# Layer 2 of a hybrid encoder: the i and z projections written as seven products of half-size quarters, with weight sums added by DMA, and the heads in groups of eight

## The chip, the core and the metric

One core of a Trainium2 chip runs the whole program. The metric is the time of one execution in microseconds (us) on the device. The engines are TensorE (PE; its weight loads are listed as PEld), VectorE (DVE), ScalarE (ACT), GpSimd (POOL) and the queue engine SyncE (SP); each works through its own instructions in a fixed order, and semaphores join them.

## What is computed

Two layers on 512 tokens of width 1024, in float32. The change lies in the second one:

```python
def odd_layer(x, norm_g, w_in, gamma_f, gamma_b, head_norm_g, w_out, layer):
    h = rms_norm(x, norm_g)                                   # 512 x 1024
    proj = h @ w_in                                           # 1024 x 10240
    q, f_f, f_b, i, z = split_cols(proj, [2048] * 5)          # 16 heads of 128 columns each
    q = jax.nn.silu(q)
    o = hgrn2(q, f_f, i, forwards) + hgrn2(q, f_b, i, backwards)
    o = o * lax.rsqrt(jnp.mean(o * o, axis=-1, keepdims=True) + EPS) * head_norm_g
    return (o * jax.nn.silu(z)) @ w_out                       # added to x, then a last rms_norm
```

## The kernel before

**Three products for one.** Every float32 operand of a main product is split into two float32r parts, hi + lo, and a product of two tiles of 128 is three matmuls, hi·hi, hi·lo and lo·hi, of 128 x 512 each. `mm3` issues them into one PSUM bank; its matmuls are the line L207 of the profile. After every eighth matmul `mm3` calls `tick()`, which lets up to three side jobs (attention, gate, recurrence of a head) each come one stage further, so that small matmuls stand between the main ones.

**Weights.** A piece is 512 KB. The class `Weights` holds the list of pieces in the order of use: `_dma` loads one on SP's queue (L49) into one of 4 buffers `wraw`, up to 7 pieces ahead of use; `_split` copies it to `whi` on ACT (L58) and subtracts to `wlo` on DVE (L59), up to 3 pieces ahead of use, 4 buffers each. A buffer `wraw` is free again when DVE has read it.

**Layer 2.** While the last products of layer 1 end tile by tile (four tiles t of 128 tokens), `norm_to_hT` squares each tile on ACT, scales it (one power on POOL, L142; two DVE products, L161), transposes it on PE (L167) and splits it into `hhi`, `hlo` (L170, L171). Then four rounds J follow. Each round has two calls of `nat_blocks`, for i and for z of four heads (512 columns): four pieces are taken, and each tile t gets 8 x 3 = 24 matmuls with all 1024 rows, so a round has 192 for i and z. `evac_i` copies the bank to `iv` on ACT (L718); `evac_z` takes a sigmoid on ACT (L721) and a product on DVE (L722). Then an output product of finished heads, and for each head three `t_block`s (q and two gates, 24 matmuls each) and the side job `hgrn`, of about 16 stages' worth of ticks. In `hgrn` POOL multiplies q (L630, L632) before the scores on PE (L642), and at the end o by z (L701).

What sets the order: the calls below are run once to build the program, a scheduler then fixes the order of each engine, and a queue never passes an instruction that waits.

## Time and profile before

| | us |
|---|---|
| median of 3 timed runs (lowest, highest) | 1036.41 (1036.37, 1037.04) |
| the profiled execution, first to last instruction | 1035.3 |
| PE busy / DVE busy / ACT busy / POOL busy | 1012.9 / 597.7 / 517.1 / 147.4 |
| main matmuls (L207), mean start to start 0.227 | 3792 |

The span leaves out 1.1 us of the timed execution. PE is the engine to watch: it is busy in 98% of the span, and its busy time is that of pipelined rows, so one matmul's listed 0.39 us is not its price; the distance from one start to the next is.

### The profile page before, as it was taken

The page shows a single profiled execution, that of the slowest core. Times are in us where ns is not written, and L with a number is a line of the kernel's source. Part 1 is how long each engine was busy: PE and PEld are TensorE (multiplying, and loading weights), DVE is VectorE, ACT ScalarE, POOL GpSimd, SP SyncE. Part 2 cuts the span into 40 slices and gives each one's busy share as a digit, 9 for nine tenths or more (in the row PEclk, how much of TensorE's full clock was granted, in tenths as well). Part 3 has the DMA queues.
Part 4 walks back from the last instruction along what each step waited for, and adds up shares of the span by engine and source line. Part 5 has one row for each costly group of instructions (what it writes and reads, how often), then busy time and mean ns, then how long its engine had stood idle before and what let it go on. Part 6 is the DMA issues. An engine that isn't in the chain of part 4 may idle for free.

```text
span 1035.3 us, 13564 instructions
## 1 busy us (share of the span) xinstructions
PE 1012.9 (98%) x5381; PEld 851.9 (82%) x5381; DVE 597.7 (58%) x946; ACT 517.1 (50%) x705; POOL 147.4 (14%) x155
## 2 busy tenths in 40 slices
PE   6999999999999999999999999999999999999996
PEld 5888888888888887888888888888888888878884
DVE  6574677566434464446754546754436764547685
ACT  5333666354222144458743258753257753377742
POOL 1140000000000200004231003322002322012101
PEclk9999999999999999999999999999999999999998
DMA  9243222222233222341212432212432223422102
GB/s 322 85 120 85 81 62 62 82 82 82 82 85 99 85 81 82 100 131 54 85 39 82 122 102 62 63 61 82 122 102 61 62 62 102 122 82 77 47 1 81
DMA packets 109343, 90.05 MB, mean 87 GB/s; under 512 B 2992, under 2 KB 88544, under 8 KB 109280
## 3 DMA queue, kind: packets, MB, share of 16 engines
q1 hardware_dynamic: 109184, 89.14, 28.3%
q8 instruction: 42, 0.69, 0.3%
q14 instruction: 21, 0.17, 0.1%
q0 software_dynamic: 96, 0.04, 0.0%
HBM read 87.08 MB, written 2.10 MB: 86 GB/s over the span
## 4 chain that ended last, share of the span: by engine, by line
PE 89%; ACT 3%; DVE 3%; issue 2%; POOL 1%; DMA 1%; SPq 0%; POOLq 0%; DVEq 0%; ACTq 0%
PE mm L207 74%; PE sm L670 2%; PE sm L642 2%; PE sm L448 1%; PE sm L685 1%; PE sm L487 1%; PE sm L691 1%; PE sm L689 1%; DVE c L614 1%; PE sm L476 1%; PE sm L658 1%; PE sm L705 1%; PE sm L512 1%; PE sm L644 1%; ACT whi L58 1%
## 5 line engine op out<-in xcount | busy, mean ns | idle before, releaser
L59 DVE TENSOR_TENSOR wlo<-wraw,whi 128x1024 fp32r<-128x1024 f32 x156 | 196.9, 1268 | 143.9 <-ACT whi L58 141.5
L58 ACT CAST whi<-wraw 128x1024 fp32r<-128x1024 f32 x156 | 163.1, 1051 | 231.2 <-PE mm L207 215.0
L207 PE MATMUL mm<-hlo,whi 128*128 128x512 f32 x656 | 258.2, 394 | 0.0
L207 PE MATMUL mm<-hhi,wlo 128*128 128x512 f32 x656 | 257.8, 393 | 0.0
L207 PE MATMUL mm<-hhi,whi 128*128 128x512 f32 x656 | 256.5, 391 | 0.0
L207 PEld LDWEIGHTS mm<-hhi,whi 128*128 128x128 f32 x656 | 123.3, 188 | 24.6
L207 PEld LDWEIGHTS mm<-hlo,whi 128*128 128x128 f32 x656 | 123.3, 188 | 24.1
L207 PEld LDWEIGHTS mm<-hhi,wlo 128*128 128x128 f32 x656 | 123.3, 188 | 23.9
L207 PE MATMUL mm<-whi,hhi 128*128 128x512 f32 (+1 forms) x352 | 135.9, 386 | 0.1
L207 PE MATMUL mm<-whi,hlo 128*128 128x512 f32 (+1 forms) x352 | 135.5, 385 | 0.0
L207 PE MATMUL mm<-wlo,hhi 128*128 128x512 f32 (+1 forms) x352 | 135.3, 385 | 0.0
L207 PE MATMUL mm<-whi,ahi 128*128 128x512 f32 x256 | 100.4, 392 | 0.1
L207 PE MATMUL mm<-wlo,ahi 128*128 128x512 f32 x256 | 100.3, 392 | 0.0
L207 PE MATMUL mm<-whi,alo 128*128 128x512 f32 x256 | 100.1, 392 | 0.0
L207 PEld LDWEIGHTS mm<-wlo,hhi 128*128 128x128 f32 x352 | 66.6, 189 | 13.1 <-DVE wlo L59 1.1
L207 PEld LDWEIGHTS mm<-whi,hhi 128*128 128x128 f32 x352 | 66.8, 190 | 12.6 <-ACT hhi L170 0.7
L207 PEld LDWEIGHTS mm<-whi,hlo 128*128 128x128 f32 x352 | 66.5, 189 | 12.0 <-DVE hlo L171 0.3
L254 DVE TENSOR_TENSOR x<-mm,x 128x512 f32<-128x512 f32 x72 | 49.0, 688 | 43.5 <-PE mm L207 43.4
L630 POOL TENSOR_TENSOR sq<-sq,en 128x512 f32<-128x512 f32 x14 | 23.8, 1700 | 266.4 <-ACT en L622 266.4
L207 PEld LDWEIGHTS mm<-whi,ahi 128*128 128x128 f32 x256 | 48.1, 188 | 10.2 <-ACT ahi L707 0.5
L207 PEld LDWEIGHTS mm<-whi,alo 128*128 128x128 f32 x256 | 48.1, 188 | 9.6
L207 PEld LDWEIGHTS mm<-wlo,ahi 128*128 128x128 f32 x256 | 48.1, 188 | 9.5
(176 smaller groups left out, 1377.2 us busy)
## 6 DMA issues: line engine op xcount, KB each, us to landing
wraw<-in_w_in_odd_dram SPq DMA_DIRECT2D x80, 512.0 KB, 3.9
wraw<-in_w_in_even_dram SPq DMA_DIRECT2D x44, 512.0 KB, 4.0
wraw<-in_w_out_even_dram SPq DMA_DIRECT2D x16, 512.0 KB, 3.5
wraw<-in_w_out_odd_dram SPq DMA_DIRECT2D x16, 512.0 KB, 3.5
x<-in_x_dram SPq DMA_DIRECT2D x4, 512.0 KB, 8.3
out_dram<-x SPq DMA_DIRECT2D x8, 256.0 KB, 2.1
pThi<-in_norm_g_even_dram SPq DMA_DIRECT2D x1, 512.0 KB, 5.4
lngb<-in_gmlp_ln_g_dram SPq DMA_DIRECT2D x1, 512.0 KB, 6.1
```

Source lines behind the costliest of these rows:

```text
L58: self.nc.scalar.copy(hi, raw)
L59: self.nc.vector.tensor_tensor(out=lo, in0=raw, in1=hi.bitcast(F32), op=ALU.subtract)
L207: nc.tensor.matmul(ps, lhsT=l, rhs=r, start=(i == 0), stop=(i == n - 1))
L254: nc.vector.tensor_tensor(out=xv, in0=ps, in1=xv, op=ALU.add)
L448: nc.tensor.matmul(pv, lhsT=a[:, ql], rhs=b[:, kv, kr], start=(i == 0), stop=(i == 2))
L476: nc.tensor.transpose(ps[:, ts(n - n0, P)], pr[:, n, ts(j - KEYS[n][0], P)], ident)
L487: nc.tensor.matmul(po[:, n0 * P:n1 * P], lhsT=a[:, j, ts(kv, P)], rhs=b[:, j, :w], start=(j == 0 and i == 0), stop=(j == NT - 1 and i == 2 ...
L512: nc.tensor.matmul(ps[:, ts(n, P)], lhsT=va[n][:, ts(c, P)], rhs=wsT[:, g], start=True, stop=True)
L614: nc.vector.tensor_tensor_scan(out=cf, data0=reset.rearrange("p n t -> p (n t)"), data1=cf, initial=0.0, op0=ALU.mult, op1=ALU.add)
L630: eng.tensor_tensor(out=v8(qb), in0=v8(qf), in1=en[:, 1, :, 0:64], op=ALU.mult)
L642: nc.tensor.matmul(ps[:H, o:o + P], lhsT=kf[:, lo_:mid], rhs=qf[:, lo_:hi_], start=True, stop=True)
L670: nc.tensor.matmul(ps[:, ts(2 * j + d, P)], lhsT=kn[:, jj, d], rhs=iv[:, n, hs], start=True, stop=True)
```

## The change

**The products.** A unit j is what a round J had: i and z of four heads, 1024 columns. Tokens, the 1024 rows and the two column halves (i, z) are each cut in two, and seven products of quarters replace eight. A product has 24 matmuls (p = 0, 1, two tiles of tokens, 12 each) and takes two new pieces; a unit has 7 x 24 = 168 instead of 192. A PSUM bank is handed on: product 1 adds onto the bank that product 0 left and that ACT or DVE has read in between (X: products 1, 2; Z: products 3, 4; Y: products 5 to 7). `unit_first` is products 1 and 2, which need only the first two tokens' tiles; `unit_rest` is 3 to 7.

**Sums of activations.** Four sums or differences of the quarters of the normed input ("forms") are made in `norm1`, which replaces `norm_to_hT` there: per p, two DVE differences from PSUM, two more in SBUF, four casts on ACT and four lo parts on DVE, plus copies on ACT. They lie in the buffers `sq`, `sg`, `c`, which the heads need; so eight DMAs of 512 KB write them to DRAM in `units(0)` and eight read them back in `units(2)`.

**Sums of weights.** Of the ten pieces of `unit_rest`, two are plain (b22), two are b12 loaded on SP with b22 added, two are b11 with b12 added ("base" of a chain, buffer `wch`), two are the same buffer with b22 added after its first split, two with b21 added after its second. Each addition is a DMA with accumulation, 512 KB, issued from POOL: 8 a unit, 32 in all. Three buffers `wch` serve eight chains.

**Order.** Two units together, then eight heads: `plan1`. The sigmoid of z now goes to a buffer `sig` and POOL multiplies. The three small loads of `rows` go from POOL's queue to SP's.

```diff
     def add(self, ap):
-        self.src.append(ap)
+        self.src.append((ap, None, None, None))
+    def add_sum(self, ap, plus, chain=None):
+        self.src.append((ap, plus, chain, False))
+    def add_grown(self, plus, chain):
+        self.src.append((None, plus, chain, True))
+    def _plus(self, t, ap):
+        self.nc.gpsimd.dma_start(out=t, in_=ap, accum_op=ALU.add)
     def _dma(self):
-        ap = self.src[self.n_dma]
-        t = self.pool.tile(list(ap.shape), F32, tag="wraw", name="wraw", bufs=self.raw_bufs)
-        self.nc.sync.dma_start(out=t, in_=ap)
-        self.raw[self.n_dma] = t
+        ap, plus, chain, grown = self.src[self.n_dma]
+        if not grown:
+            tag, bufs = ("wch", self.chain_bufs) if chain is not None else ("wraw", self.raw_bufs)
+            t = self.pool.tile(list(ap.shape), F32, tag=tag, name=tag, bufs=bufs)
+            self.nc.sync.dma_start(out=t, in_=ap)
+            if plus is not None:
+                self._plus(t, plus)
+            self.raw[self.n_dma] = t
         self.n_dma += 1
     def _split(self):
         i = self.n_split
-        raw = self.raw.pop(i)
+        _, _, chain, grown = self.src[i]
+        raw = self.chains.pop(chain) if grown else self.raw.pop(i)
         hi = self.pool.tile(list(raw.shape), F32R, tag="whi", name="whi", bufs=self.bufs)
         lo = self.pool.tile(list(raw.shape), F32R, tag="wlo", name="wlo", bufs=self.bufs)
         self.nc.scalar.copy(hi, raw)
         self.nc.vector.tensor_tensor(out=lo, in0=raw, in1=hi.bitcast(F32), op=ALU.subtract)
         self.ready[i] = (hi, lo)
         self.n_split += 1
+        if chain is not None:
+            later = next((p for _, p, c, g in self.src[i + 1:] if c == chain and g), None)
+            if later is not None:
+                self._plus(raw, later)
+                self.chains[chain] = raw
...
+    W.chain_bufs = 3
...
-    def mm3(ps, ops):
+    def mm3(ps, ops, first=True):
         n = len(ops)
         for i, (l, r) in enumerate(ops):
-            nc.tensor.matmul(ps, lhsT=l, rhs=r, start=(i == 0), stop=(i == n - 1))
+            nc.tensor.matmul(ps, lhsT=l, rhs=r, start=(first and i == 0), stop=(i == n - 1), skip_group_check=not first)
...
-    for J in range(4):
-        add_nat(wio, OI1 + J * 512)
-        add_nat(wio, OZ1 + J * 512)
-        if J:
-            add_out(woo, 4 * (J - 1), 2 if J == 3 else 4)
-        for h in range(4 * J, 4 * J + 4):
-            add_tcols(wio, OQ1 + h * P)
-            add_tcols(wio, OF1 + h * P)
-            add_tcols(wio, OB1 + h * P)
+    def quarter(j, kh, nh):
+        c0 = (OI1, OZ1)[nh] + j * 512
+        return [cols(wio[(512 * kh + 256 * p):(512 * kh + 256 * p + 256)], c0, 512) for p in range(2)]
+    def add_unit_first(j):
+        for ap in quarter(j, 0, 0) + quarter(j, 1, 0):
+            W.add(ap)
+    def add_unit_rest(j):
+        b11, b12, b21, b22 = quarter(j, 0, 0), quarter(j, 0, 1), quarter(j, 1, 0), quarter(j, 1, 1)
+        for p in range(2):
+            W.add_sum(b11[p], b12[p], (j, p))
+        for p in range(2):
+            W.add(b22[p])
+        for p in range(2):
+            W.add_grown(b22[p], (j, p))
+        for p in range(2):
+            W.add_sum(b12[p], b22[p])
+        for p in range(2):
+            W.add_grown(b21[p], (j, p))
+    plan1 = [("units", 0), ("heads", 0, 6), ("out", 0, 4), ("heads", 6, 8), ("units", 2), ("heads", 8, 10), ("out", 4, 4), ("heads", 10, 14),
+             ("out", 8, 2), ("heads", 14, 16)]
+    for kind, *i in plan1:
+        if kind == "units":
+            add_unit_first(i[0])
+            add_unit_first(i[0] + 1)
+            add_unit_rest(i[0])
+            add_unit_rest(i[0] + 1)
+        elif kind == "heads":
+            for h in range(*i):
+                add_head(h)
+        else:
+            add_out(woo, *i)
...
-        nc.gpsimd.dma_start(out=rows[32 * d:32 * d + 32], in_=gsrc.rearrange("l (h d) -> (l h) d", d=P))
-    nc.gpsimd.dma_start(out=rows[64:80], in_=hng[0].rearrange("(h d) -> h d", d=P))
+        nc.sync.dma_start(out=rows[32 * d:32 * d + 32], in_=gsrc.rearrange("l (h d) -> (l h) d", d=P))
+    nc.sync.dma_start(out=rows[64:80], in_=hng[0].rearrange("(h d) -> h d", d=P))
...
+    FORM_TAGS = ("sq", "sq", "sq", "sg", "sg", "sg", "c", "c")
+    def form_tiles():
+        f = [l1.tile([P, 4, 256], F32R, tag=g, name="form", bufs=2 if g == "c" else 3) for g in FORM_TAGS]
+        return [(f[2 * i], f[2 * i + 1]) for i in range(4)]
+    forms = form_tiles()
+    r1 = l1.tile([P, 2, 2, 512], F32, tag="zv", name="r1", bufs=2)
+    formed = set()
+    def norm1(t, g, h, ss, wait):
+        p = t % 2
+        r = rstd_halves(ss, "nr")
+        for kq, cs in enumerate(halves):
+            nc.vector.scalar_tensor_tensor(out=h[:, cs], in0=xs[t][:, cs], scalar=r, in1=g[kq], op0=ALU.mult, op1=ALU.mult)
+        yield wait
+        if t >= 2:
+            r22 = l1.tile([P, 512], F32, tag="o2", name="r22", bufs=1)
+            s1 = l1.tile([P, 512], F32, tag="u", name="s1", bufs=1)
+            s3 = l1.tile([P, 512], F32, tag="kn1", name="s3", bufs=1)
+        for kq in (0, 1) if t < 2 else (1, 0):
+            ps = sm_bank()
+            for j in range(4):
+                nc.tensor.transpose(ps[:, ts(j, P)], h[:, ts(4 * kq + j, P)], ident)
+            pv = ps.rearrange("p (j t) -> p j t", j=4)
+            hv = hhi[:, 4 * kq:4 * kq + 4, ts(t, P)]
+            nc.scalar.copy(hv, pv)
+            nc.vector.tensor_tensor(out=hlo[:, 4 * kq:4 * kq + 4, ts(t, P)], in0=pv, in1=hv.bitcast(F32), op=ALU.subtract)
+            if t < 2:
+                nc.scalar.copy(r1[:, p, kq], ps)
+            elif kq == 1:
+                nc.scalar.copy(r22, ps)
+            else:
+                nc.vector.tensor_tensor(out=s1, in0=ps, in1=r22, op=ALU.subtract)
+                nc.vector.tensor_tensor(out=s3, in0=ps, in1=r1[:, p, 0], op=ALU.subtract)
+        normed.add(t)
+        if t < 2:
+            return
+        s2, s4 = r1[:, p, 0], r1[:, p, 1]
+        nc.vector.tensor_tensor(out=s2, in0=s1, in1=s2, op=ALU.subtract)
+        nc.vector.tensor_tensor(out=s4, in0=s4, in1=s2, op=ALU.add)
+        for i, sgn, src in ((0, 1.0, s1), (3, 1.0, s4), (1, 1.0, s2), (2, -1.0, s3)):
+            hi, lo = (f[:, :, ts(p, P)] for f in forms[i])
+            sv = src.rearrange("p (j t) -> p j t", j=4)
+            nc.scalar.activation(hi, sv, AF.Copy, scale=sgn)
+            nc.vector.scalar_tensor_tensor(out=lo, in0=sv, scalar=sgn, in1=hi.bitcast(F32), op0=ALU.mult, op1=ALU.subtract)
+        formed.add(p)
...
-            spawn(norm_to_hT(t, g1, ht[:, t % 2], sst[t], 2))
+            spawn(norm1(t, g1, ht[:, t % 2], sst[t], 2))
...
+    def a_quarter(kh, th):
+        return lambda k, p: [a[:, 4 * kh + k, ts(2 * th + p, P)] for a in (hhi, hlo)]
+    def a_form(i):
+        return lambda k, p: [f[:, k, ts(p, P)] for f in forms[i]]
+    def product(a_of, banks, first, done):
+        pieces = [W.take() for _ in range(2)]
+        for p in range(2):
+            if first:
+                tick_until(lambda: p in normed)
+                banks.append(mm_bank())
+            ops = []
+            for k in range(4):
+                (a, b), (whi, wlo) = a_of(k, p), pieces[k // 2]
+                ops += [(a, whi[:, k % 2]), (a, wlo[:, k % 2]), (b, whi[:, k % 2])]
+            mm3(banks[p], ops, first)
+            done(p, banks[p])
+    def sub(out, a, b):
+        nc.vector.tensor_tensor(out=out, in0=a, in1=b, op=ALU.subtract)
+    def unit_first(iv):
+        X = []
+        product(a_quarter(0, 0), X, True, lambda p, ps: nc.scalar.copy(iv[:, 2 + p], ps))
+        product(a_quarter(1, 0), X, False, lambda p, ps: nc.scalar.copy(iv[:, p], ps))
+    def unit_rest(iv, zv):
+        def silu(t):
+            sig = l1.tile([P, 512], F32, tag="o2", name="sig", bufs=1)
+            nc.scalar.activation(sig, zv[:, t], AF.Sigmoid)
+            nc.gpsimd.tensor_tensor(out=zv[:, t], in0=zv[:, t], in1=sig, op=ALU.mult)
+        def c12(p, ps):
+            sub(zv[:, p], zv[:, p], ps)
+            silu(p)
+        def c22(p, ps):
+            sub(zv[:, 2 + p], zv[:, 2 + p], ps)
+            silu(2 + p)
+        Z, Y = [], []
+        product(a_form(0), Z, True, lambda p, ps: sub(zv[:, 2 + p], ps, iv[:, 2 + p]))
+        product(a_form(3), Z, False, lambda p, ps: sub(zv[:, p], ps, iv[:, 2 + p]))
+        product(a_form(1), Y, True, c12)
+        product(a_form(2), Y, False, c22)
+        product(a_quarter(1, 1), Y, False,
+                lambda p, ps: nc.vector.tensor_tensor(out=iv[:, 2 + p], in0=ps, in1=iv[:, 2 + p], op=ALU.add))
+    ivs, zvs = {}, {}
+    spill = ctx.enter_context(tc.tile_pool(name="spill", bufs=1, space=bass.MemoryType.DRAM))
+    kept = [[spill.tile([P, 4, 256], F32, name=f"form{i}{j}", tag=f"form{i}{j}") for j in range(2)] for i in range(4)]
+    def units(j):
+        nonlocal forms
+        for k in (j, j + 1):
+            ivs[k] = l1.tile([P, NT, 512], F32, tag="iv", name="iv", bufs=2)
+            unit_first(ivs[k])
+        if j:
+            forms = form_tiles()
+            for f, d in zip(forms, kept):
+                for a, b in zip(f, d):
+                    nc.sync.dma_start(out=a.bitcast(F32), in_=b)
+        else:
+            tick_until(lambda: len(formed) == 2)
+            for f, d in zip(forms, kept):
+                for a, b in zip(f, d):
+                    nc.sync.dma_start(out=b, in_=a.bitcast(F32))
+        for k in (j, j + 1):
+            zvs[k] = l1.tile([P, NT, 512], F32, tag="zv", name="zv", bufs=2)
+            unit_rest(ivs[k], zvs[k])
+    def heads(h0, h1):
+        for h in range(h0, h1):
             sq = l1.tile([P, 2, S], F32, tag="sq", name="sq", bufs=3)
             sg = l1.tile([P, 2, S], F32, tag="sg", name="sg", bufs=3)
             ps = t_block()
             for d in range(2):
                 ps = t_block()
                 nc.scalar.activation(sg[:, d], ps, AF.Sigmoid)
-            spawn(hgrn(h, sq, sg, iv, zv))
+            spawn(hgrn(h, sq, sg, ivs[h // 4], zvs[h // 4]))
+    def outs(k0, n):
+        tick_until(lambda: all(k in acat1 for k in range(k0, k0 + n)))
+        out_blocks([acat1[k] for k in range(k0, k0 + n)])
+    for kind, *i in plan1:
+        {"units": units, "heads": heads, "out": outs}[kind](*i)
...
-    nc = _bacc.Bacc("TRN2", target_bir_lowering=False, num_devices=1)
+    nc = _bacc.Bacc("TRN2", target_bir_lowering=False, num_devices=1, dynamic_dma_scratch_size=2048)
```

Three places show how it moves the engines' rows. In the names, `wraw` and `wch` are raw weights, `whi`, `wlo` their parts, `form` a form, `s`, `r` its float32 sources.

DVE where tile 3 (`x_73`) is normed, at the start of layer 2. Before:

```order
L254 TENSOR_TENSOR x_73<-mm,x_73 128x512
L59 TENSOR_TENSOR wlo<-wraw,whi 128x1024
L155 TENSOR_SCALAR nrv<-ss 128x1
L161 SCALAR_TENSOR_TENSOR ht<-x_73,nrr,gain_3031 128x512 x2
L171 TENSOR_TENSOR hlo<-sm,hhi 128x4x128 x2
```

The same engine and place after the change:

```order
L278 TENSOR_TENSOR x_73<-mm,x_73 128x512
L681 TENSOR_TENSOR s_3240<-sm,r_3239 128x512
L682 TENSOR_TENSOR s_3241<-sm,r_3042 128x512
L77 TENSOR_TENSOR wlo<-wraw,whi 128x1024
L687 TENSOR_TENSOR r_3042<-s_3240,r_3042 128x512
L693 SCALAR_TENSOR_TENSOR form<-s_3240,form 128x4x128
L688 TENSOR_TENSOR r_3042<-r_3042 128x512
L693 SCALAR_TENSOR_TENSOR form<-r_3042,form 128x4x128
L77 TENSOR_TENSOR wlo<-wraw,whi 128x1024
L693 SCALAR_TENSOR_TENSOR form<-r_3042,form 128x4x128
L693 SCALAR_TENSOR_TENSOR form<-s_3241,form 128x4x128
L179 TENSOR_SCALAR nrv<-ss 128x1
```

Eight instructions of tile 2's forms and a second weight split now stand between tile 3's last sum and its norm.

POOL from the end of layer 1's norms on. Before:

```order
L142 TENSOR_TENSOR nrr<-nrv,mhalf 128x1 x4
L630 TENSOR_TENSOR sq<-sq,en 128x512
L632 TENSOR_TENSOR sq<-sq,c 128x512
L606 MEMSET c 128x16
L651 TENSOR_TENSOR asum<-asum,ax 64x4x64 x2
```

The same after the change (L57 is the accumulating DMA, L853 the product with the sigmoid):

```order
L166 TENSOR_TENSOR nrr<-nrv,mhalf 128x1 x4
L57 DMA wraw<-in_w_in_odd_dram 128x2x512 x2
L57 DMA wch<-in_w_in_odd_dram 128x2x512 x4
L57 DMA wraw<-in_w_in_odd_dram 128x2x512
L853 TENSOR_TENSOR zv<-zv,sig 128x512
L57 DMA wraw<-in_w_in_odd_dram 128x2x512
L853 TENSOR_TENSOR zv<-zv,sig 128x512 x2
L57 DMA wch<-in_w_in_odd_dram 128x2x512
L853 TENSOR_TENSOR zv<-zv,sig 128x512
L57 DMA wch<-in_w_in_odd_dram 128x2x512 x5
```

Nothing stood on POOL between the norms and the first head's products; now fourteen accumulating DMAs and four products with the sigmoid stand in these rows.

SP's queue at the same place. Before:

```order
L49 DMA wraw<-in_w_out_even_dram 128x2x512 x8
L49 DMA wraw<-in_w_in_odd_dram 128x2x512 x2
L585 DMA gain_3031<-in_norm_g_odd_dram 128x1024
L49 DMA wraw<-in_w_in_odd_dram 128x2x512 x6
L49 DMA wraw<-in_w_in_odd_dram 128x8x128 x12
```

The same after the change:

```order
L64 DMA wraw<-in_w_in_odd_dram 128x2x512 x9
L889 DMA form_3273<-form 128x1024
L889 DMA form_3277<-form 128x1024
L889 DMA form_3274<-form 128x1024
L889 DMA form_3275<-form 128x1024
L889 DMA form_3276<-form 128x1024
L889 DMA form_3278<-form 128x1024
L889 DMA form_3279<-form 128x1024
L889 DMA form_3280<-form 128x1024
L64 DMA wraw<-in_w_in_odd_dram 128x2x512 x4
L64 DMA wch<-in_w_in_odd_dram 128x2x512 x2
```

The eight writes of forms stand before the plain pieces of unit 1 and before the base of the fourth chain, the first of the two `wch` at the end. (The bases of the first three chains are loaded, and summed, far ahead, in layer 1.)

## Rows read from the trace of the kernel before

**Rows 1.** The page: span, and busy time (share of span) and instructions by engine.

```profile
span 1035.3 us, 13564 instructions
...
PE 1012.9 (98%) x5381; PEld 851.9 (82%) x5381; DVE 597.7 (58%) x946; ACT 517.1 (50%) x705; POOL 147.4 (14%) x155
```

**Rows 2.** Waits of PE: waiting line, releaser: us in total, times, longest.

```profile
PE sm L167 <- DVE h L161: 8.2, 3, 7.5
PE sm L642 <- POOL sq L632: 4.1, 4, 1.0
```

**Rows 3.** Timeline of PE in dense main products: start us, us, instruction.

```profile
354.77 0.39 PE L207 MATMUL mm<-whi,alo 128*128 128x512 f32 x1
...
371.77 0.39 PE L207 MATMUL mm<-whi,alo 128*128 128x512 f32 x1
```

**Rows 4.** Windows: length, busy by engine (instructions), granted clock, DMA share, GB/s.

```profile
0.00:25.90 25.90, 17.60 (x73) 13.10 (x74) 16.24 (x25) 14.06 (x27) 3.34 (x12) 1.00 0.90 322
...
393.10:437.60 44.50, 44.24 (x199) 36.02 (x198) 16.10 (x20) 15.94 (x24) 0.55 (x1) 1.00 0.31 94
...
440.00:520.00 80.00, 78.97 (x469) 66.54 (x468) 49.26 (x75) 56.42 (x66) 18.76 (x19) 1.00 0.31 93
```

**Rows 5.** Timeline around tile 3's norm, DVE.

```profile
395.87 0.68 DVE L254 TENSOR_TENSOR x<-mm,x 128x512 f32<-128x512 f32 x1
396.46 1.22 DVE L59 TENSOR_TENSOR wlo<-wraw,whi 128x1024 fp32r<-128x1024 f32 x1
397.60 0.21 DVE L155 TENSOR_SCALAR nrv<-ss 128x1 f32<-128x1 f32 x1
398.46 1.42 DVE L161 SCALAR_TENSOR_TENSOR ht<-x,nrr,gain 128x512 f32<-128x512 f32 x2 [0.66 <-POOL nrr L142]
```

**Rows 6.** Timeline around tile 3's norm, PE.

```profile
392.35 1.03 PE L167 MATMUL sm<-ident,ht 128*128 128x128 f32 x8
393.14 0.48 PE L207 MATMUL mm<-whi,hhi 128*128 128x512 f32 x1
...
399.36 1.29 PE L167 MATMUL sm<-ident,ht 128*128 128x128 f32 x8 [0.21 <-DVE ht L161]
```

**Rows 7.** Groups by line: busy us, mean ns | idle before, releasers.

```profile
L59 DVE TENSOR_TENSOR wlo<-wraw,whi 128x1024 fp32r<-128x1024 f32 x156 | 196.9, 1268 | 143.9 <-ACT whi L58 141.5
L58 ACT CAST whi<-wraw 128x1024 fp32r<-128x1024 f32 x156 | 163.1, 1051 | 231.2 <-PE mm L207 215.0 <-issue 12.6 <-DMA wraw<-in_w_in_even_dram 3.0
...
L722 DVE TENSOR_TENSOR zv<-mm,zv 128x512 f32<-128x512 f32 x16 | 11.0, 690 | 42.4 <-ACT zv L721 42.4
...
L161 DVE SCALAR_TENSOR_TENSOR ht<-x,nrr,gain 128x512 f32<-128x512 f32 x8 | 5.7, 748 | 2.4 <-POOL nrr L142 2.4
...
L542 POOL DMA_DIRECT2D rows<-in_hgrn_gamma_fwd_dram x1 | 0.7, 725 | 0.0
```

**Rows 8.** DMA issues: transfer, queue, count, KB each, median us to landing.

```profile
wraw<-in_w_in_odd_dram SPq DMA_DIRECT2D x80, 512.0 KB, 3.9
...
x<-in_x_dram SPq DMA_DIRECT2D x4, 512.0 KB, 8.3
```

**Rows 9.** The tile zv on POOL: ns min/median/max of one, first and last start.

```profile
L701 POOL TENSOR_TENSOR o<-o,zv x14: 1288/1308/2140, 489.3 to 973.4; 128x512 f32<-128x512 f32 x14
```

More of the change, by code (lines that the diff above doesn't have):

```diff
@@ L40, in __init__ @@
         self.src, self.raw, self.ready = [], {}, {}
+        self.chains = {}
         self.n_dma = self.n_split = self.n_used = 0
     def add(self, ap):
[L44 to L50 removed]
+        self.src.append((ap, None, None, None))
[5 more added lines that the diff above has]
+        self.nc.gpsimd.dma_start(out=t, in_=ap, accum_op=ALU.add)
+    def _dma(self):
+        ap, plus, chain, grown = self.src[self.n_dma]
[6 more added lines that the diff above has]
+            self.raw[self.n_dma] = t
         self.n_dma += 1
@@ L711, in hgrn @@
         yield 1
-    for J in range(4):
-        iv = l1.tile([P, NT, 512], F32, tag="iv", name="iv", bufs=2)
-        zv = l1.tile([P, NT, 512], F32, tag="zv", name="zv", bufs=2)
-        def evac_i(t, ps):
-            nc.scalar.copy(iv[:, t], ps)
-        def evac_z(t, ps):
-            nc.scalar.activation(zv[:, t], ps, AF.Sigmoid)
-            nc.vector.tensor_tensor(out=zv[:, t], in0=ps, in1=zv[:, t], op=ALU.mult)
-        nat_blocks(evac_i)
-        nat_blocks(evac_z)
-        if J:
-            n = 2 if J == 3 else 4
-            tick_until(lambda: 4 * (J - 1) + n - 1 in acat1)
-            out_blocks([acat1[4 * (J - 1) + k] for k in range(n)])
-        for h in range(4 * J, 4 * J + 4):
+    def a_quarter(kh, th):
+        return lambda k, p: [a[:, 4 * kh + k, ts(2 * th + p, P)] for a in (hhi, hlo)]
```

4 lines of the change are left out of this document (added).

## Prediction

> **What bounds the kernel now.** I read the page's first part before anything else: PE is busy in 1012.9 of 1035.3 us and no other engine passes 58% [rows 1]. PE's busy time overlaps itself, so the second view is its waits: apart from 8.2 us at the very start, only 4.1 us in four waits stand against it in the whole span [rows 2]. So nearly every microsecond is a matmul's turn, and a matmul that goes is time that goes. The third view gives its price: between two rows 75 matmuls apart lie 371.77 - 354.77 = 17.00 us, 0.2267 us each [rows 3]. The listed 0.39 us is not the price. The other engines and the DMA engines cost nothing now because they have room: in the i and z block of round J = 0, 44.5 us, DVE works 16.1, ACT 15.9, POOL 0.6, and the DMA engines are 31% busy [rows 4]. That room is what the change spends. The question is whether PE stays fed.
>
> **The change, part by part.**
>
> *Matmuls.* Four units save 24 each: 96 x 0.2267 = **-21.8 us**. No other PE work is added, and the form operands have the tile shapes of the old ones, so I keep the price.
>
> *Starts of a run of heads.* The four waits of PE for POOL's product of q, 1.0 us each, come where a run of heads begins with no earlier head in flight [rows 2]; there are four rounds. Now only heads 0 and 8 begin so: **-2.0 us** (bounds 0 and -2.0).
>
> *Norm of tile 3.* Today DVE ends the tile's last sum at 396.55, has one split, and starts nrv at 397.60, ht at 398.46 [rows 5]; PE transposes at 399.36, 0.9 us after ht begins [rows 6]. Now eight form instructions come in between, four at 0.69 and four at 0.75 (prices of L722 and L161 [rows 7], 5.8 us), a second split of 1.27, and about 0.6 us for a cast on ACT that DVE needs: nrv at 405.2. Another split stands between nrv and ht, so ht starts 1.5 us later, 406.7, and the transposes at 407.6. PE arrives there 56 matmuls after 393.14 [rows 6], at 405.8. Everything behind it on PE waits: **+1.7 us**. The remaining forms have 41 matmuls, 9.3 us, until the first product needs them; by the same prices that is enough.
>
> *Splits and evacuations.* A unit has 14 pieces and now uses one per 12 matmuls (2.7 us) instead of 24. DVE: 14 x 1.27 + 10 x 0.69 = 24.7 us in the unit's 168 x 0.2267 = 38.1, 65%; ACT about 51% [rows 7]. Both fit. They are queues, though, and a bank must be read within 12 matmuls before the next product adds to it. For the resulting short waits I put **+1.5 us** (0 to 3). The heads run denser than before only in number: in a stretch of heads today DVE is at 62%, ACT at 71% [rows 4], and that rate just continues.
>
> *The accumulating DMA.* No row shows one. Call L its time from issue to landing. Nearest rows: a plain 512 KB load lands in 3.9 us, and in 8.3 in the crowded start [rows 8]. The start moves 322 GB/s at 90% share [rows 4], so full rate is 358 GB/s and 512 KB hold the engines 1.46 us. If the destination is read as well, 1.46 more: 5.4 alone, and 6 with some company, which I take. Ends: 3.9 (accumulating is free), and 8.3 + 1.5, about 10. The Trainium skill ("DMA: Bandwidth & Descriptors", Anatomy of one DMA — SWDGE (gpsimd) path) gives for a plain load issued from GpSimd 2.0 us plus bytes over 436 GB/s, an estimate of 3.2 here; with it the sum below would be -17.6. No run here shows it.
>
> *Grown pieces.* A chain's buffer returns to DVE four pieces, 48 matmuls or 10.9 us, after its last split. In it lie ACT's cast 1.05, DVE's 1.27 [rows 7] and the issue on POOL, 0.7 (the DMA row of POOL [rows 7]), so L may be 7.9 us. At L = 6 they cost **0**.
>
> *The fourth chain.* This is the place I worry about, in units(0) and again in units(2). With three buffers, its base is loaded only after the first chain's last split. Let S be the start of unit_rest and P = 24 x 0.2267 = 5.44 us one product. That split follows both subtractions of the third product on DVE: it ends at S + 3P + 0.7 + 1.3. Load 3.9, issue 0.7, L, cast and split 2.3: ready at S + 3P + 8.9 + L. PE wants it six matmuls into the second unit's rest, S + 5P + 1.4 = S + 3P + 12.3. The wait is L - 3.4: 2.6 us at L = 6, twice, **+5.2 us** (0.5 each at 3.9, 6.6 at 10). Queued behind it: on DVE and ACT the following splits, on POOL the next accumulations, on SP the bases of units(2).
>
> *Writing the forms.* Eight writes, 4.2 MB, 11.7 us at 358 GB/s, stand on SP ahead of unit 1's plain pieces and of that base, while POOL's accumulations run. I put **+3.0 us** in units(0) (0 if the writes end in time, 6 if half of them lies in the way). In units(2) the reads of the forms come earlier, beside the last two heads' side work, so 0. The Trainium skill ("DMA: Bandwidth & Descriptors", Issuing engines are not separate DMA queues) says that POOL's and SP's transfers run on the same 16 engines and interleave. If POOL's had a path of their own, this term would go and the sum would be -15.4.
>
> *Early and late.* Three bases and their sums lie in layer 1, where the queues have room; the moved `rows` loads and the end of the program I cost at 0. A slower clock after a wait I don't price: the longest wait, 7.5 us, lies in a stretch whose granted clock is 1.00, the 2.4 GHz level [rows 2, 4].
>
> **Sum:** -21.8 - 2.0 + 1.7 + 1.5 + 5.2 + 3.0 = -12.4 us. On the profiled execution, 1035.3 - 12.4 = 1022.9 span, plus the 1.1 us around it: **1024.0 us**.
>
> **Rivals.**
>
> *All hidden.* L is 3.9, the writes and the queues cost nothing: -21.8 - 2.0 + 1.7 + 1.0 = -21.1, 1015.3 us. For it: DMA engines at 31% [rows 4]. Against it: three stages of transfers in one chain.
>
> *The accumulation is the bound (slower).* At L = 10 the fourth chain costs 2 x 6.6 = 13.2; its two grown links, with no lead left, 2.1 each, four in all, 8.4; the writes 6, the queues 3: -21.8 - 2.0 + 1.7 + 13.2 + 8.4 + 6 + 3 = +8.5, **1044.9 us**. The other chains live on their lead of three pieces. For it: in the two rests of units(0) (54.4 us) I count 8 writes, 6 loads and 12 accumulations; at double price for the latter that is 38 x 0.524 MB = 19.9 MB, 366 GB/s, 102% of the full rate, and then L grows by itself. Against it: at single price it is 70%. With these terms the sum passes zero at L = 8.6, close to the 8.3 of the crowded start [rows 8]. Between 7.5 and 8.6 the gain is nearly eaten: about 1035.
>
> *Handing on the banks.* If both splits of a product stand ahead of a subtraction, it ends 2 x 1.27 + 0.69 = 3.2 us after its bank, 0.5 beyond the 12 matmuls. A unit has 8 such banks, 32 in all: 16 us in place of 1.5, +2.1, 1038.5 us. Against it: the order of DVE mostly alternates split and subtraction.
>
> *POOL's products with the sigmoid.* The same product takes 1.3 to 2.1 us today [rows 9], and they stand between accumulations on POOL. At 2.1 instead of 1.3, three ahead of the late base, at most 2.6 us twice: this is inside the range.
>
> **How the numbers follow.** Forecast (L from 4.5 to 7.5; 1017 to 1032): 0.50. All hidden: 0.13. Nearly eaten (1032 to 1039): 0.10. Accumulation the bound: 0.19. Banks: 0.08. The range 1015 to 1043 leaves out half of the slow case and a little of the hidden one. About 0.2%, 2 us, is what a measurement of this kernel can tell from no change. Faster by more: 0.50 + 0.13 + 0.05 + 0.02 = 0.70; within: 0.05 + 0.04 = 0.09; slower: 0.19 + 0.02 = 0.21.
>
> **What would show it.** 3696 main matmuls at 0.227. A wait of PE near 406 for ht, 1 to 3 us. A wait for whi or wlo of the fourth chain at the second rest of each units call; its size plus 3.4 is L, and the transfers' median to landing can be read beside it (4.5 to 7.5). Waits elsewhere inside the rests, for whi from `wch`, mean that L passes 7.9; waits of the products' first matmuls for DVE's subtractions mean the banks; two waits of the scores for POOL instead of four. I am wrong if accumulations land after 8.6 us, or if other engines hold PE in the heads.

## The result, and the profile after

The changed kernel takes **1052.7 us** (median of 4; 1051.6 to 1053.2) against 1036.7 before: ratio 1.0152, 95% interval 1.0138 to 1.0167. The forecast was 1024.0 with a range from 1015 to 1043: the sign is wrong, and the time lies 9.7 us above the range. (The span below leaves out 1.7 us of its own execution, 1053.2; the 1.1 given for the kernel before sets its span against a median. The forecast is a difference and isn't touched.)

The page of the kernel after: span, busy time by engine, two rows of the 40 slices (26.3 us each) and the two DMA queues (packets, MB, share of the 16 engines' time).

```profile
span 1051.5 us, 13681 instructions
...
PE 1003.1 (95%) x5285; PEld 838.9 (80%) x5285; DVE 654.7 (62%) x1010; ACT 550.4 (52%) x744; POOL 210.0 (20%) x200
...
PEclk9999999999999999889999999999999999999998
DMA  9742221322332227999322222457873232231102
...
q1 hardware_dynamic: 113792, 101.77, 30.9%
q0 software_dynamic: 8704, 16.78, 9.2%
```

Against [rows 1], PE is busy 9.8 us less (21.8 were to go), and the span is 16.2 longer: PE stands idle for 48.4 us instead of 22.4. The DMA row says where to look: it holds a 9 from 420 to 500 us (slices 16 to 18, counted from 0), which is most of units(0), and PEclk falls to 8 in two of them. The last two lines hold the price that matters, though it is easily passed over: q0, GpSimd's queue, carries the 32 accumulations, 16.78 MB, in 9.2% of 1051.5 us = 96.7 us of all 16 engines, **5.8 us a MB**; q1 carries the plain transfers at 30.9% for 101.77 MB, **3.2 us a MB**.

The longest waits of PE (in total, times, longest):

```profile
PE mm L231 <- DVE zv L842: 9.2, 1, 9.2
PE mm L231 <- ACT whi L76: 9.2, 2, 5.4
PE sm L191 <- DVE h L185: 8.0, 2, 7.5
PE sm L747 <- POOL sq L737: 4.1, 4, 1.0
PE sm L790 <- POOL asum L756: 3.0, 1, 3.0
```

The third is the start of the program, as in [rows 2]. The first names DVE's subtraction, but DVE wasn't slow. The chain of work that ended last, with its start and length in us, shows what stood ahead of it:

```profile
414.31 16.93 DMA wch<-in_w_in_odd_dram
...
431.34 1.05 ACT whi L76
...
432.42 1.23 DVE wlo L77
433.64 0.61 DVE zv L842
...
434.30 10.19 PE mm L231 x36
...
453.58 7.57 DMA wch<-in_w_in_odd_dram
...
461.22 1.05 ACT whi L76
...
462.30 1.24 DVE wlo L77
...
463.58 36.52 PE mm L231 x148
```

The first grown piece was issued at 414.31 and landed 16.9 us later. Its cast, its split and, behind the split in DVE's queue, the subtraction that frees a bank follow it, and PE waits 9.2 us. The second block is the fourth chain: 7.6 us to landing and 5.4 of waiting. What comes behind each wait is dear, too: 36 matmuls in 10.19 us are 0.283 each, not 0.2267 [rows 3]. The windows (length, busy by engine, granted clock, DMA share, GB/s) show the clock. The DMA share adds up the packets' time on the 16 engines and can pass 1.00:

```profile
393.10:492.00 98.90, 83.10 (x344) 66.32 (x344) 59.67 (x73) 47.29 (x63) 31.60 (x27) 0.91 0.91 228
...
420.00:430.00 10.00, 5.11 (x23) 3.79 (x21) 0.27 (x1) 0.00 (x0) 1.19 (x1) 0.87 1.08 294
430.00:440.00 10.00, 5.70 (x18) 4.58 (x19) 4.64 (x5) 4.22 (x5) 2.39 (x2) 0.62 1.02 282
...
434.30:439.30 5.00, 5.00 (x15) 4.02 (x16) 2.11 (x3) 2.50 (x3) 1.46 (x2) 0.67 1.08 306
439.30:444.30 5.00, 5.00 (x23) 4.00 (x22) 3.18 (x4) 3.63 (x4) 0.74 (x1) 1.00 0.80 153
```

PE stands still until 434.3, so 4.3 of the 10 us at 0.62 cost no matmul. When it starts again, the granted clock is at the lower of its two levels, 1.2 GHz: in the next 5 us the mean is 0.67 and 15 matmuls pass, in the 5 us behind them it is 1.00 and 23 pass. The first line is the whole of units(0): 336 products' matmuls, worth 76.2 us, take 98.9, with the DMA engines 91% busy.

The median times from issue to landing (KB each, us):

```profile
wraw<-in_w_in_odd_dram SPq DMA_DIRECT2D x80, 512.0 KB, 4.1
...
wch<-in_w_in_odd_dram POOLq DMA_DIRECT2D x24, 512.0 KB, 7.0
...
form<-form SPq DMA_DIRECT2D x16, 512.0 KB, 4.8
wch<-in_w_in_odd_dram SPq DMA_DIRECT2D x8, 512.0 KB, 6.7
wraw<-in_w_in_odd_dram POOLq DMA_DIRECT2D x8, 512.0 KB, 8.8
```

The accumulating ones take 7.0 and 8.8 us in the median; each by itself in units(0), from 5.5 to 16.9. Plain ones take 4.1, against 3.9 in [rows 8].

### The profile page after: what moved, and what is told of

It reads as the page before. It is cut to its first block, busy times and chain, and to the rows that moved or that the text cites. A ratio compares the mean times of both kernels' runs of the same rounds, so it can differ in the third digit from the quotient of the medians.

```text
span 1051.5 us, 13681 instructions
## 1 busy us (share of the span) xinstructions
PE 1003.1 (95%) x5285; PEld 838.9 (80%) x5285; DVE 654.7 (62%) x1010; ACT 550.4 (52%) x744; POOL 210.0 (20%) x200
## 3 DMA queue, kind: packets, MB, share of 16 engines
q1 hardware_dynamic: 113792, 101.77, 30.9%
q0 software_dynamic: 8704, 16.78, 9.2%
## 4 chain that ended last, share of the span: by engine, by line
PE 79%; DVE 6%; ACT 5%; DMA 4%; issue 3%; POOL 2%; SPq 0%; POOLq 0%; DVEq 0%; ACTq 0%
PE mm L231 65%; DMA wch<-in_w_in_odd_dram 3%; PE sm L775 2%; PE sm L747 2%; DVE wlo L77 1%; PE sm L503 1%; PE sm L542 1%; PE sm L790 1%; DVE c L719 1%; ACT whi L76 1%; PE sm L796 1%; PE sm L794 1%; PE sm L531 1%; ACT L727 1%; PE sm L763 1%
## 5 line engine op out<-in xcount | busy, mean ns | idle before, releaser
L77 DVE TENSOR_TENSOR wlo<-wraw,whi 128x1024 fp32r<-128x1024 f32 x156 | 199.2, 1283 | 120.6 <-ACT whi L76 119.3
L76 ACT CAST whi<-wraw 128x1024 fp32r<-128x1024 f32 x156 | 163.4, 1052 | 185.0 <-PE mm L231 167.6
L231 PE MATMUL mm<-whi,form 128*128 128x512 f32 x256 | 87.1, 417 | 18.4 <-DVE zv L842 9.2
L231 PEld LDWEIGHTS mm<-whi,form 128*128 128x128 f32 x256 | 51.3, 201 | 32.0 <-ACT whi L76 10.1
L231 PE MATMUL mm<-whi,hhi 128*128 128x512 f32 (+1 forms) x192 | 73.4, 383 | 1.4 <-ACT iv L846 1.1
L231 PE MATMUL mm<-wlo,hhi 128*128 128x512 f32 (+1 forms) x192 | 72.8, 380 | 0.0
L231 PE MATMUL mm<-whi,hlo 128*128 128x512 f32 (+1 forms) x192 | 72.7, 379 | 0.0
L572 POOL TENSOR_TENSOR za<-za,mxd 128x512 f32<-128x512 f32 x8 | 10.3, 1293 | 269.3 <-DVE mxd L569 269.3
L77 DVE TENSOR_TENSOR wlo<-wch,whi 128x1024 fp32r<-128x1024 f32 x24 | 32.5, 1362 | 45.5 <-ACT whi L76 45.5
```

The lines of the kernel that those rows point to most:

```text
L76: self.nc.scalar.copy(hi, raw)
L77: self.nc.vector.tensor_tensor(out=lo, in0=raw, in1=hi.bitcast(F32), op=ALU.subtract)
L231: nc.tensor.matmul(ps, lhsT=l, rhs=r, start=(first and i == 0), stop=(i == n - 1), skip_group_check=not first)
```

## Experiments

Time before in all of them: 1036.5 to 1036.9 us. The theories are named in the expectations: A, the DMA engines are full because accumulating costs them more; B, only the meeting of the form writes with the first grown pieces hurts; C, the order of DVE's queue. (Where two texts say 28 accumulations, it is 32; where 16 are counted in the first stage, 14 are issued there, since three sums of bases lie in layer 1.)

**1. no_sums and plain_copy: what the accumulations cost.**

```
-        self.nc.gpsimd.dma_start(out=t, in_=ap, accum_op=ALU.add)
+        pass                                      # no_sums
+        self.nc.gpsimd.dma_start(out=t, in_=ap)   # plain_copy
```

> The 28 accumulating transfers are left out, and with them the weight sums; every matmul, split and evacuation stays. This is the floor of the accumulations. Theory A: 46.6 us of the engines' time go in the first stage, what is left (loads 10.5 MB and writes 4.2 MB, 45 us) lies under 76 us of matmuls: 1019 us (1015 to 1025), the sum of the prediction without its transfer terms, and the wait of 9.2 us is gone. Theory B: the first two grown pieces have no transfer to wait for either, 9.2 us, some 5 us of the fourth chain and the slower clock go: 1025 to 1032. Theory C: stops of 1 to 3 us stay at each late split: 1035 to 1045.

> The 28 accumulating transfers become plain transfers of the same bytes, from the same queue, at the same places and with the same waits; the second summand overwrites the first, so the weight sums are left out. Theory A (the transfer engines are full in the first units stage, because an accumulating byte costs them more): between 395 and 470 us the accumulating queue took 46.2% of 75 us for 6.23 MB, 5.6 us a MB, the other queue 45.0% for 11.15 MB, 3.0 us a MB; the stage has 16 accumulations, 8.39 MB, so plain ones take 2.5 x 8.39 = 21 us off some 91 us that the stage asks of the engines, under the 76.2 us of its matmuls. Most of the stops go: 1024 us (1018 to 1032), landing under 6 us in the median. Theory B (only the eight writes of forms falling on the first two accumulations hurt; the accumulation as such is cheap): the writes are still there, the 9.2 us wait shrinks by 3 at most: 1046 to 1050. Theory C (the order of VectorE's instructions, late splits ahead of a bank's subtraction): no change, 1050 to 1053.

no_sums: **1020.5 us** (1020.3 to 1020.9). plain_copy: 1037.9 (1031.4 to 1044.2 in ten runs; the profiled one spans 1032.0). First no_sums: page, and a window on its first units stage; then plain_copy: queues, and the window from 420 us.

```profile
span 1019.2 us, 13582 instructions
...
PE 994.0 (98%) x5285; PEld 834.0 (82%) x5285; DVE 655.2 (64%) x1010; ACT 550.1 (54%) x744; POOL 171.6 (17%) x168
...
393.10:471.60 78.50, 77.73 (x343) 63.22 (x342) 60.76 (x72) 46.78 (x63) 13.36 (x11) 1.00 0.60 193
```

```profile
q1 hardware_dynamic: 113792, 101.77, 31.6%
q0 software_dynamic: 4608, 16.78, 5.1%
...
420.00:430.00 10.00, 6.91 (x27) 5.30 (x26) 3.24 (x4) 2.09 (x2) 0.73 (x1) 0.89 1.02 415
```

Without the transfers the stage takes 78.5 us, DVE is as busy over the program as in the changed kernel (C falls), and only tile 3's norm waits in it. So 1052.7 - 1020.5 = **32.1 us** come with the accumulations, all that the change would have won and 16 more: in the two profiled runs 32.3, of which 23.2 are PE's idle time (48.4 against 25.2) and 9.1 busy time of the same 5285 instructions (1003.1 against 994.0). The busy time is the clock's: read in windows of 1 us, behind four waits (9.2, 5.4, 3.0 and 3.8 us) PE works at the lower level, and busy time times the missing share of the clock adds up to 8.9 us; no_sums has no such window. plain_copy moves the same bytes from the same queue with the same waits; only `accum_op` is gone, and the queue's price falls from 5.8 to 52.6 / 16.78 = 3.1 us a MB. From 420 to 430 us the engines are full in both kernels, at shares of 1.08 and 1.02, and move 294 and 415 GB/s. That gives back 14.8 us; the transfers as such keep the other 17.3. With runs that spread over 13 us this division is a rough one. A's transfers land as forecast, under 6 us in the median, but its time of 1018 to 1032 is missed, as is every other: by these medians the adding is about half of the loss, not most of it.

**2. writes_after, writes_between, writes_held and one_write: the form writes.** The first two move the loop of the writes in the code, behind the second or the first unit's rest:

```
         for k in (j, j + 1):
             ...
             unit_rest(ivs[k], zvs[k])
+        if not j:
+            for f, d in zip(forms, kept):
+                ...
```

> The eight writes of the forms are issued after the last product of the first units stage instead of ahead of its second half. Theory A: the stage asks 13 us less of the transfer engines (4.19 MB at 3.0 us), 78 us against 76 us of matmuls: 1040 us (1036 to 1043), and waits for the fourth chain stay at 4 to 6 us. Theory B: the 9.2 us wait goes whole, with 2 us of matmuls at the lower clock and the waits that followed: 1033 to 1037. Theory C: no change, 1050 to 1053. If head 0 has to wait for its buffers behind the writes, up to 5 us come back in any of them.

> The eight writes are issued between the two second halves of the first units stage: away from the first two grown pieces, but still inside the stage. Theory A: the sum of what the stage asks of the engines is the same 91 us, only the place of the stop moves, to the second unit's pieces: 1048 us (1044 to 1053). Theory B: the first 9.2 us wait goes; the writes now meet the second unit's accumulations, which had 7.6 us to landing, but theory B takes those as far enough ahead: 1036 to 1042. Theory C: no change, 1050 to 1053.

1051.6 (1049.3 to 1052.0) and 1052.6 us (1050.8 to 1055.2): no change, but both tell nothing, because the writes had not moved. SP's timeline of writes_after (start, length):

```profile
411.92 6.59 SPq L893 DMA_DIRECT2D form<-form  x5
418.61 2.90 SPq L64 DMA_DIRECT2D wraw<-in_w_in_odd_dram  x2
421.56 4.55 SPq L893 DMA_DIRECT2D form<-form  x3
```

The scheduler issues a write as soon as its form is there, wherever the code has it. The next two make it certain: writes_held gives SP a fixed order in the stage, one_write leaves seven writes out.

```
+            with tc.manual_schedule(engines={mybir.EngineType.SP}):   # writes_held
+                unit_rest(ivs[k], zvs[k])
+                if k == 1: ...the eight writes

-            for f, d in zip(forms, kept): ...                          # one_write
+            nc.sync.dma_start(out=kept[0][0], in_=forms[0][0].bitcast(F32))
```

> In the last two runs the writes had not moved: the scheduler issued them as soon as the forms were there (412 to 426 us), wherever the code stood. Here the loads of the first units stage keep the order in which they are written, and the eight writes come after the stage's last load. Theory A (transfer engines full in the stage): 13 us of their time leave the stretch from 412 to 490 us, where they are full: 1040 us (1035 to 1044), the first wait under 5 us. Theory A2 (full only because each accumulating transfer is slow in its own queue, one after the other, whoever else is on the engines): the first grown piece still lands 12 to 15 us after its issue: 1047 to 1052. Theory B (the writes meet the first two grown pieces): 1033 to 1037.

> Seven of the eight writes of forms are left out, and the second units stage reads the one kept block eight times, so its products are of the wrong forms; transfers, sizes and waits of the second stage stay. In writes_held the loads of the stage stood in written order behind a load that waited 30 us for a buffer, which confounds it; here nothing else moves. Theory A (transfer engines full in the stage): 3.67 MB x 3.0 = 11 us of their time go: 1040 us (1036 to 1044), the first wait under 4 us, the fourth chain's 4 to 6 us stay. Theory A2 (accumulating transfers are slow one after the other, whoever else is there): the first grown piece still takes over 10 us: 1047 to 1052. Theory B (the meeting of writes and grown pieces is all): 1033 to 1037.

writes_held 1050.4 (1049.8 to 1052.7), one_write 1046.0 (1045.3 to 1047.4). B falls: with one write left, 6.6 us come back, not 16 to 19. A's 1040 is missed too, by 6. A2, by which accumulations are slow in their own queue whoever else is there, comes nearest in time (1047 to 1052). The chain of one_write shows why, and behind it its DMA queue from 416 to 422 us:

```profile
418.69 10.08 DMA wch<-in_w_in_odd_dram
...
446.44 7.08 DMA wch<-in_w_in_odd_dram
...
453.60 1.05 ACT whi L76
...
q0 software_dynamic: 624, 1.21, 112.1%
```

A grown piece takes 10.1 us with hardly a write beside it: four accumulations were issued between 412 and 421, and 4 x 0.52 x 5.8 = 12 us of the engines' time is what they share. In those 6 us no other queue moves anything, and the accumulations alone fill the engines with 0.2 MB a us. Yet A2's ground doesn't hold: the first grown piece lands after 16.9 us with the writes, 9.4 in one_write and 8.5 in writes_held, so it does matter who else is there. The 9.2 us wait shrinks to 2.0; the fourth chain's stays, 5.6 after 5.4. writes_held has a fault of its own: in a fixed order, loads queued for 30 us behind one that waited for a buffer.

**3. chain4: a fourth buffer for growing pieces**, `W.chain_bufs = 4`.

> A fourth buffer for growing pieces, so that the last chain of a stage doesn't wait for the first one's buffer. The prediction put 2.6 us on that wait twice; the trace shows 5.4 and 3.8 us of stop plus matmuls at the lower clock behind each. Theory D (the wait is the buffer's): 9 to 14 us less: 1038 to 1044. Theory A (the engines are full, what is loaded earlier takes its time from the pieces ahead): the stop moves, 1048 to 1053.

1045.7 us (1045.5 to 1046.7), **7.0 less** than the changed kernel with the same bytes at the same price. The 9.2 us wait stays (9.1 here). So the place of a transfer counts beside the load, and D is only partly right: it asked for 9 to 14.

**4. add_pool, add_dve, add_dve_free: an engine adds.** The second summand is loaded plainly, with a fifth raw buffer to hold it. The first two hold the writes as above.

```
+        r = self.pool.tile(list(plus.shape), F32, tag="wraw", ...)
+        self.nc.sync.dma_start(out=r, in_=plus)
+        self.nc.gpsimd.tensor_tensor(out=t, in0=t, in1=r, op=ALU.add)   # add_pool; nc.vector in the others
```

> The same sums without accumulating transfers: the second summand comes as a plain load into a fifth raw buffer, and GpSimd adds it (32 additions of 128x1024; the one such shape in the trace, va, took 3.1 us). The writes are held as in writes_held. Theory A: the stage asks 18.9 MB of loads at 3.0 us, 57 us, and no writes, under 76 us of matmuls; GpSimd has 16 x 3.1 = 50 us of additions in 76 us, and its queue holds the sigmoid products too: stops of 1 to 3 us at some of the sums remain: 1026 us (1020 to 1036). Theory E (GpSimd as the next bound, in order with the sigmoid products and the scores' additions): 1036 to 1050.

> As add_pool, with VectorE adding: 16 additions a stage at about 1.2 us (a subtraction of that size takes 1.28 us), 20 us more on an engine that has 49 of 80 us in use there. Theory A: 1024 us (1019 to 1032), below add_pool because an addition is 1.9 us shorter and GpSimd's queue is free. Theory C (VectorE's order is what stops PE): each addition waits for a load and holds the banks' subtractions behind it: 1036 to 1050, slower than add_pool.

> As add_dve, but the writes go where the scheduler puts them (412 us on) and the loads keep no fixed order. Theory F (add_dve lost its gain to the fixed order, loads queued behind one that waits for a buffer): 1026 to 1032. Theory A with VectorE as the second bound (its stops of 1 to 3 us at the banks' subtractions): 1034 to 1040, no difference to add_dve, the writes' 13 us being hidden now.

add_pool **1062.2** (1058.9 to 1063.3), add_dve 1036.0 (1034.0 to 1039.0), add_dve_free 1035.8 (1034.2 to 1037.4; ratio 0.9995, 0.9985 to 1.0004). GpSimd is the worst place by far, beyond E's 1036 to 1050 as well. Its group of additions, and DVE's splits beside it:

```profile
L88 DVE TENSOR_TENSOR wlo<-wraw,whi 128x1024 fp32r<-128x1024 f32 x156 | 227.6, 1465 | 121.8 <-ACT whi L87 120.9
L77 POOL TENSOR_TENSOR wch<-wch,wplus 128x1024 f32<-128x1024 f32 x24 | 70.8, 2961 | 34.2 <-DMA wplus<-in_w_in_odd_dram 15.7 <-DVE wlo L88 10.0 <-issue 6.8
```

One addition takes 2.96 us there and 1.28 on DVE, and DVE's 156 splits of that program become slower, 1465 ns against 1283 (1299 with the additions on DVE, in add_dve_free). add_dve wins back 16.7 us of the 32. Fixing SP's order or not makes no difference (F falls). A's 1019 to 1032 is missed; add_dve lies at the edge of C's range, though far under add_pool and not above it, and add_dve_free where DVE as a second bound was put. The stops that are left are short, 3.3 us at most, but DVE is busy for up to 10 in 10 us of the stage.

**5. grown_dve, grown_dve_c4: only the growing is added by DVE**, with three and with four chain buffers.

> The base sums stay accumulating transfers; the growing of a chain, which must wait for its last split, becomes an early plain load into a fifth raw buffer and an addition on VectorE. 8 of 16 accumulations in a stage are left: 4.19 MB x 2.5 = 10.6 us of the transfer engines' time go, and VectorE gets 8 x 1.25 = 10 us. Theory A: 1029 us (1023 to 1036), no wait over 4 us in the first stage. Theory G (it is the latency of the accumulation between two splits, not the sum of transfers): 1024 to 1030, and the share of transfers stays near 1.0 without stops. Theory C (VectorE's order): 1036 to 1046, as add_dve or slower.

> As grown_dve, with four buffers for growing pieces and four raw ones (loads six pieces ahead instead of seven). Theory D (the fourth chain's wait is its buffer's): 3 to 8 us under grown_dve. Theory A: the smaller lookahead costs what the buffer brings: within 3 us of grown_dve.

1042.4 (1041.7 to 1043.7) and 1037.0 (1036.1 to 1038.8). The first lies above A's and G's ranges and within C's, but its longest wait isn't DVE's: in it a sum, b12 + b22, still accumulating, became the late piece (issued at 431.2, landed 7.6 us later), and PE waits 4.5 us for its cast. The fourth buffer is worth 5.4 us here, although it took the place of a raw one, as D had it (3 to 8).

**6. keep_acc, keep_dve, keep_last: fewer transfers.** The pieces of b22 stay in their raw buffers, of which there are five. DVE adds them to the chain, then adds b12 onto them; b21 is loaded plainly and added to the chain by DVE.

```
-            W.add(b22[p])
+            W.add_keep(b22[p], (j, p))
-            W.add_grown(b22[p], (j, p))
+            W.add_grown(None, (j, p))          # chain += the kept piece, on DVE
-            W.add_sum(b12[p], b22[p])
+            W.add_onto(b12[p], (j, p))         # the kept piece += b12, on DVE
```

keep_acc leaves a chain's first sum accumulating, 8 in the program; keep_dve leaves none; keep_last leaves 6: the last chain of each stage is added by DVE.

> The pieces of b22 stay in their raw buffers: VectorE adds them to the chain, then adds b12 onto them for the next sum. Only the first sum of a chain is an accumulating transfer. A unit moves 12 plain pieces of 0.52 MB and 2 accumulating ones instead of 10 and 8, VectorE makes 6 additions of 1.25 us a unit. Theory A (load of the transfer engines): the stage asks 12.6 MB x 3.0 + 2.1 x 5.6 + 13 for writes = 62 us, under 76 us of matmuls; no stop over 2 us: 1027 us (1022 to 1033). Theory G (an accumulation that stands between two splits is what stops PE): the same, no accumulation stands there. Theory C (VectorE's queue as the bound, 49 + 15 us in 80): 1034 to 1040, as add_dve.

> As keep_acc, with the first sum of a chain on VectorE too: 14 plain pieces a unit, no accumulating transfer, 8 additions a unit. Theory A: 14.7 MB x 3.0 + 13 = 57 us asked, 1025 to 1033, at or a little under keep_acc. Theory C: 2.5 us more of VectorE's time a unit, 1035 to 1041, 1 to 4 us over keep_acc; and the same as add_dve_free although 12.7 us of transfers are gone from each stage.

> As keep_acc, but the first sum of the last chain of each stage is made by VectorE; two accumulating transfers of eight become additions. In keep_acc that transfer took 6.96 us between the landing of the base (439.9) and the split (447.5), and 5.81 us in the second stage. Theory G (an accumulation on the path costs its time to landing less an addition): up to 5.7 and 4.6 us earlier, of which the stops there (1.8 us and the subtractions behind, 2.8 us of idle between 440 and 450, 3.3 us between 450 and 460 in all) can come back: 1028 to 1031. Theory C (VectorE's queue takes it back): 1032 to 1035.

> The same kernel as keep_acc, beside keep_last: 1031 to 1034, faster than the kernel before by 0.25 to 0.5%.

keep_acc 1032.9 (1030.6 to 1034.6; 0.9962, 0.9950 to 0.9973), keep_dve 1033.1 (1032.7 to 1035.0), **keep_last 1026.1** (1025.1 to 1027.3; ratio **0.9900, 0.9886 to 0.9914**). The second run of keep_acc, beside keep_last: 1032.2, as expected. In keep_acc's chain one accumulation is left, and it stands between a base that waited for its buffer and a split:

```profile
435.41 4.49 DMA wch<-in_w_in_odd_dram
...
440.52 6.96 DMA wch<-in_w_in_odd_dram
...
447.55 1.05 ACT whi L92
```

keep_last replaces it, one transfer a stage, by an addition of 1.2 us. Its page and its PE timeline from 392 to 480 us, the rows with a wait:

```profile
span 1025.5 us, 13640 instructions
...
PE 997.1 (97%) x5285; PEld 834.5 (81%) x5285; DVE 686.6 (67%) x1036; ACT 549.2 (54%) x744; POOL 182.5 (18%) x174
```

```profile
406.76 1.06 PE L682 MATMUL sm<-ident,ht 128*128 128x128 f32 x8 [0.77 <-DVE ht L673]
441.03 0.50 PE L242 MATMUL mm<-wlo,hhi 128*128 128x512 f32 x1 [0.16 <-DVE wlo L93]
442.76 0.49 PE L242 MATMUL mm<-whi,hhi 128*128 128x512 f32 x1 [0.29 <-DVE zv L853]
447.76 0.50 PE L242 MATMUL mm<-wlo,form 128*128 128x512 f32 x1 [0.32 <-DVE wlo L93]
```

Apart from the norm of tile 3, no wait in the first stage passes 0.32 us. The engines' price of two transfers, 2 x 0.52 x 2.6 = 2.7 us, can't give the 6.1 us between 1032.2 and 1026.1, so most of it is their place; the time is better than G's 1028 to 1031. keep_dve doesn't gain over keep_acc: PE waits 7.1 us for DVE's splits and subtractions there against 2.3, with DVE busy to 10 in 10 us over long stretches. That fits C, more weakly than C said, but no run tests it alone. keep_last beats both kernels.

## Why the prediction was wrong, point by point

- **Matmuls, -21.8.** The 96 instructions went, all others kept their price: no_sums is 16.3 us under the kernel before, and the prediction's sum without the fourth chain's 5.2 would have been 1018.8. In busy time PE shows -18.9; where the other 2.9 went, I didn't find.
- **Starts of a run of heads, -2.0: wrong.** There are still four waits, 4.1 us. They end at 524, 684, 821 and 889 us: a run of heads also starts afresh behind the output products (heads 6 and 10), which I had counted only at the units.
- **Norm of tile 3, +1.7.** Right in place, 0.8 us in size: the wait at 406.6.
- **Splits and evacuations, +1.5; the bank rival.** Right: no_sums has one wait of 1.1 us for such work and none for a bank's subtraction. The 9.2 us that name one are a late transfer's.
- **L, the step that failed.** I took 6 us, a latency: 5.4 alone, for two passes over 512 KB, and "some company". The 5.4 was right, 5.5 is the shortest in units(0); the company was not. The price of 5.8 / 3.2 = 1.8 times a plain byte is about the double that I counted, but with up to four accumulations and the writes in flight a piece lands after up to 17 us. My own slow rival had the count, 102% of the full rate at double price, "and then L grows by itself"; the 91% of units(0), 102 to 108% around the longest wait, is what it described. I should have asked that sum of the stage first, and taken a single transfer's time only if it came out well under 100%. The accumulations' term was +5.2; with the clock behind their waits it measured **+32.1**. The Trainium skill ("Collectives: The Full Stack", Stop ④ — SDMA + CCE: where bytes move and the add happens) says of a collective's transfers that the DMA path adds while the bytes stream through: two reads and a write, the add free in between. No engine did the adding here either: DVE's busy time is the same without the transfers (655.2, 654.7), and POOL's extra 38.4 us are 32 issues at 1.2. What such a transfer costs the DMA engines is measured here, 5.8 against 3.1 us a MB; no run separates the second read from the add.
- **Grown pieces, 0.** Wrong with L: the 16.9 us of the first one is past the 7.9 that were free, and made the longest wait.
- **The fourth chain.** Right as a place: ending at 462.3 and 759.3, 5.4 and 3.8 us. By its formula L - 3.4 the measured L of 7.6 gives 4.2. chain4 shows the buffer's part, 7.0 us.
- **The form writes, +3.0.** About twice that: 6.6 us (one_write). They are not the main cause, though the trace of the changed kernel alone suggests it, since they stand beside the longest wait. The page named there on the shared engines (the Trainium skill, "DMA: Bandwidth & Descriptors", Issuing engines are not separate DMA queues) is borne out: without seven of SP's writes POOL's first grown piece lands after 9.4 us, not 16.9.
- **POOL.** One rival had its sigmoid products at 2.6 us twice. They do stand between accumulations on the fourth chain's path, and the accumulations' issues, 1.2 us each rather than the 0.7 I took, hold back a score's addition: 3.0 us at 716.
- **The clock, not priced.** I argued from the wait at the program's start that no clock is lost, since the row of that stretch says 1.00. Inside a dense stage the granted clock fell in the waits, and the same instructions took 9.1 us more busy time. The trace of the kernel before had the sign, 4 us behind that very wait:

```profile
11.56 0.63 PE L207 MATMUL mm<-whi,hhi 128*128 128x512 f32 x1
11.99 0.63 PE L207 MATMUL mm<-wlo,hhi 128*128 128x512 f32 x1
12.42 0.63 PE L207 MATMUL mm<-whi,hlo 128*128 128x512 f32 x1
```

The starts are 0.43 us apart, nearly twice 0.2267 and about what they are at 0.50 behind 434.3 (8 matmuls in 3.2 us), although the clock row reads 1.00 there.

- **The chances.** The slow rival had 0.19 and 1044.9 us. Its mechanism was the right one; it lacked the clock and the meeting with the writes in the two first grown links.

What stays open: how the 17.3 us that plain_copy leaves divide between the bytes and the waits' places. chain4 (7.0) and keep_last (6.1) show the places' part only at two loads. Why plain_copy's runs spread over 13 us is open.

## What to carry to other kernels

Before a transfer's latency goes into a sum, add up what its stage asks of all DMA engines, each kind at its own price, against the stage's length; near 100% no latency of a quiet row held here. A sum of weights was cheaper as a plain load and an addition on DVE, which had room, and cheaper still where one operand was already in SBUF. Accumulating transfers that PE hardly waits for were better left: keep_last has six of them and is 7 us faster than keep_dve, which has none. A wait's named releaser is the last in a queue: follow the chain back to what stood ahead of it before moving anything.
